# Three fills moved ahead in one scan stage, loads put behind a store, and the low part of the latent stages' weights made by a negated copy and an accumulating DMA

## The chip, the cores and the metric

The kernel runs on one core of a Trainium2 chip. Its metric is the device time of one execution in microseconds; the text gives the median of several executions. The engines are TensorE (PE, with its weight loads as PEld), VectorE (DVE), ScalarE (ACT), GpSimd (POOL) and SyncE (SP). SP and POOL issue the DMA transfers that matter here.

## The reference, cut to what matters

Two layers work on 512 latent tokens of 1024 channels, with 256 context tokens in front. The even layer has an RWKV-7 scan in both directions and a gated short convolution side by side:

```python
rc, kc, vc, zac, bc, cc, xc, zbc = jnp.split(hc @ w_in, EVEN_SPLITS, axis=-1)
yac, S_f, S_b = rwkv_seq(rwkv_prep(hc, ...), zero, zero, ...)      # the context: final states only
r, k, v, za, bg, cg, xb, zb = jnp.split(h @ w_in, EVEN_SPLITS, axis=-1)
ya, _, _ = rwkv_seq(rwkv_prep(h, r, k, v, ...), S_f, S_b, ...)     # the latent tokens
yb = bg * dwconv(cg * xb, sc_w, seg_len)
y = jnp.concatenate([ya * silu(za), yb * silu(zb)], axis=-1) @ w_out
```

Per token and head the scan does `S = S * w + (S @ -kk) (kk * a)^T + v k^T` and reads `S @ r`. The odd layer is a gated convolution of 31 taps with layer norm. Each layer is `x + gate * rms_norm(y)`, with shift, scale and gate from `silu(c) @ mod_w + mod_b`. Everything is fp32.

## The kernel before

*Exactness.* A product of fp32 matrices is made of three matmuls in a faster 32-bit format (`mm3`, every matmul of the trace is on line 57): each operand is split into a high part, a copy in that format, and a low part, the operand less the high part. For weights `hilo` does it: SP loads 128x512 fp32 (`wr...`, a half of a 1024x128 block of `w_in`), ACT copies it to `wh...` (line 129), DVE subtracts into `wl...` (line 130). `w_half` gives the buffers: two raw ones, three for each part. `load_w` loads both halves of a block, `proj` multiplies, 24 matmuls of 128x512 a block. The names end in the block and the half: `wlbg51` is the low part of half 1 of block `bg` 5.

*Stages.* The scan is done in chunks, as matmuls. Twelve stages follow a prologue: s=0 to 3 run the chain of the context's head groups (`chain_ctx`, four chunks), s=4 to 11 that of the eight latent groups (`chain_lat`, eight chunks). The chain is serial; after it in the text of a stage stands the work for coming stages, one letter each in `STAGE`: `O` the outputs of the next group (`po`), `S` its triangular solve (`solve`, in halvings on DVE with `Xl`, `Yl`, `xtmpl`), `M` the merge of the solved blocks on PE and DVE (`kdml`, `aml`, `Pml`, `uh`), `P` projections and the LoRA parts for the group after next (`prep_lat`), `L` the decays and keys (`light`, `ARl`, `BKl`, `kdl`), `H` its products within a chunk (`heavy`: `pal` masked by DVE into `E`, line 682, then `pbl` copied by ACT into `BKt`, line 695), `F` projections kept for later in DRAM (`fills`, through `psp`) and, from s=4, the group's end (`finish`: `Ol`, `osq`, `orq`, `ysp`), `C` one group of the short convolution (`conv_branch(s-3)`: blocks `cg`, `xb`, `bg` and the gate `zb`).

*Order.* A scheduler orders each engine's instructions by dependencies, by the order of the text, and by the text's anchors: `after(x)` and `issue_after(x)` let an instruction start in the order only behind `x`; `anchored` does so with a chunk of the chain. In `conv_branch` the weights' loads and their matmuls are anchored to chunks 0, 2, 7 and 6 of the chain. Each engine then runs its queue strictly in order. `rest` is the odd layer's (and the gate's) modulation, 17 steps laid between other work: of four matmuls each, on 128 rows of `mod_w` in four tiles of 512 columns; it loads the next group into the same tiles (`home`) from POOL. `between()` and `inner` are the places where a step may stand. `project` stores its result by POOL to `psp`.

*Names in the trace.* The trace leaves buffer numbers out, and one `pal` or `zoc` row of an engine's order stands for two of its records.

Of the kernel before, what the change touches and what calls it, by code (L numbers as in the profile page):

```python
# [15 lines left out]
P = 128  # L16
# [15 lines left out]
CONV_AFTER = (0, 2, 7, 6)  # L32
PA_ORDER = ((0, 1), (1, 0), (1, 1), (0, 0))
HEAVY = ("ANB", "ANBV")
STAGE = ("KLSMVHvF", "OPLSMHF", "OSPLMHFC")
FILL_R = (0, 0, 2, 3, 4, 4, 4, 4)
FILL_Z = (0, 1, 1, 1, 3, 3, 3, 3)
ZR = (slice(0, 64), slice(64, 128))
# [13 lines left out]
def kernel(ctx: ExitStack, tc: tile.TileContext, I: dict, out: bass.AP):  # L52
# [63 lines left out]
    w_in = I["ev_w_in"][0]  # L116
    wo = I["ev_w_out"][0]
    ORDER = list(range(8, 16)) + list(range(8))
    env = {"lo": V, "first": False}

    def bank(name, tag):
        return ps.tile([P, 512], F32, tag=tag, name=name, bufs=2 if tag in ("at", "zo") else 1)
# [255 lines left out]
    def lora(hp, w1, between):  # L378
        pwl, pal = (ps.tile([P, 512], F32, tag="zo", name=n, bufs=2) for n in ("pwl", "pal"))
        pwc = ps_at("pwc")  # L380
        for kt in range(KT):
            h1 = hp[kt][:, 1:771]
            dh = w("AR", f"dh{kt}")[:, 0:770]
            V.tensor_tensor(out=dh, in0=hp[kt][:, 0:770], in1=hp[kt][:, 2:772], op=ALU.add)
            for (zi, pl) in ((0, pwl), (1, pal)):
                xw = E1[:, (2 * kt + zi) % 4 * D : (2 * kt + zi) % 4 * D + 770]
                S.activation(xw, h1, AF.Copy, scale=owa[:, zi * 8 + kt : zi * 8 + kt + 1])
                V.scalar_tensor_tensor(out=xw, in0=dh, scalar=hwa[:, zi * 8 + kt : zi * 8 + kt + 1], in1=xw,
                                       op0=ALU.mult, op1=ALU.add)
                lhs = w1[zi][kt // 4][:, kt % 4].rearrange("p a b -> p (a b)")  # L390
                mm(pl, lhs, xw[:, 258:770], kt == 0, kt == KT - 1)
                mm(pwc[:, zi * CTX : (zi + 1) * CTX], lhs, xw[:, 0:CTX], kt == 0 and zi == 0, kt == KT - 1 and zi == 1)
            if kt % 2:
                between()
        lorl.extend([cvp.tile([P, SEQ], F32R, tag=f"{t}{z}", name=f"{t}{z}") for z in range(2)] for t in ("tanhl", "xal"))
        S.activation(lorc[0], pwc[:, 0:CTX], AF.Tanh)
        S.copy(lorc[1], pwc[:, CTX : 2 * CTX])
        for i, pl in enumerate((pwl, pal)):
            t, th = w("tmp", f"lor{i}"), w("tmp", f"lorh{i}", F32R)
            S.activation(t, pl, AF.Copy if i else AF.Tanh)  # L400
            S.copy(th, t)
            for z in range(2):
                rows, hr, lr = (slice(64 * x, 64 * x + 64) for x in (z, i, 1 - i))
                S.copy(lorl[i][z][hr], th[rows])
                V.tensor_tensor(out=lorl[i][z][lr], in0=t[rows], in1=th[rows], op=ALU.subtract)
# [4 lines left out]
    def w_half(src, name):  # L410
        raw = wp.tile([P, 512], F32, tag="wr", name="wr" + name, bufs=2)
        hi, lo = (wp.tile([P, 512], F32R, tag="w" + x, name=f"w{x}{name}", bufs=3) for x in "hl")
        with tc.high_priority() if env["first"] else nullcontext():
            return hilo(src, raw, hi, lo)

    def early_w(cb, raw):
        res = []
# [25 lines left out]
    def project(p, which, rc=None, between=None):  # L443
        nm = "rkv"[which] + str(p)
        wt = first_w.pop(nm) if nm in first_w else load_w(which * 8 + p, nm)
        if rc is not None:
            pc = (ps_at if nm in ("k0", "k1") else ps_mm)("pc" + nm)[:, :CTX]
            proj(wt, pc, (hch, hcl))
            shifted(pc, rc, p, which)
            if between:  # L450
                between()
        pl = ps_mm("pl" + nm)
        proj(wt, pl, hlat)
        flip["at"] ^= 1
        tag = ("cg", "yb")[flip["at"]]
        rl = cvp.tile([P, SEQ], F32, tag=tag, name="l" + nm)
        shifted(pl, rl, p, which)
        nc.gpsimd.dma_start(psp[p, which], rl)

    def state(lat, x):  # L460
        ps_ = [x] if lat else [2 * x, 2 * x + 1]
# [4 lines left out]
    def prep_ctx(b, between=None, st=None, kinds=(1, 2), inner=None, js=(0, 1)):  # L466
        st = st or state(False, b)
        for which in kinds:
            nm = "rkv"[which]
            if nm not in st:  # L470
                st[nm] = w("r_" if which == 1 and b % 2 else nm + "_", nm + st["nm"])
            for p, cs in [st["parts"][j] for j in js]:
                project(p, which, st[nm][:, cs], inner)
                if between:
                    between()
        return st
# [185 lines left out]
    def heavy(st, an=None):  # L662
# [5 lines left out]

        def pa():
            for gi, (z, g) in enumerate(PA_ORDER if lat else ((0, 0), (1, 0))):  # L670
                with anchored(an, ha[gi if lat else 2 * gi]):
                    AR, BK = st["AR"][z], st["BK"][z]
                    m, x = (4, P) if lat else (8, CH)
                    c0 = m * g
# [232 lines left out]

    def conv_branch(p, an=None):
        anchors = [None if an is None or x is None else an[x] for x in ((0, 2, 4, 6) if p == 7 else CONV_AFTER)]
        with after(anchors[0]):  # L910
            wt = load_w(40 + p, f"cg{p}")
            pcg = ps_mm(f"pcg{p}")
            proj(wt, pcg, hlat)
        cg = cvp.tile([P, SEQ], F32, tag="cg", name=f"cg{p}")
        S.copy(cg, pcg)
        with after(anchors[1]):
            wt = load_w(48 + p, f"xb{p}")
            pxb = ps_mm(f"pxb{p}")
            proj(wt, pxb, hlat)
        V.tensor_tensor(out=cx[:, :, 1:65], in0=ch3(pxb), in1=ch3(cg), op=ALU.mult)  # L920
        yb = cvp.tile([P, SEQ], F32, tag="yb", name=f"yb{p}")
        S.activation(ch3(yb), cx[:, :, 0:64], AF.Copy, scale=hc("sc_w", p))
        for j in (1, 2):
            V.scalar_tensor_tensor(out=ch3(yb), in0=cx[:, :, j : j + 64], scalar=hc("sc_w", 8 * j + p),
                                   in1=ch3(yb), op0=ALU.mult, op1=ALU.add)
        with after(anchors[2]):
            wt = load_w(32 + p, f"bg{p}")
            pbg = ps_mm(f"pbg{p}")
            proj(wt, pbg, hlat)
        V.tensor_tensor(out=yb, in0=pbg, in1=yb, op=ALU.mult)  # L930
        with after(anchors[3]):
            gz = gate(p, 56, "zb")
        V.tensor_tensor(out=yb, in0=yb, in1=gz, op=ALU.mult)
        nc.gpsimd.dma_start(ysp[8 + p], yb)
# [15 lines left out]
    def rest():  # L950
# [16 lines left out]
        for g in ((n + 1,) if n else (0, 1)):  # L967
            for q in ((0, 1, 2, 3), (3, 2, 1, 0))[g % 2] if g < 16 else ():
# [4 lines left out]
                    with tc.issue_after(env["last"].ins):  # L973
                        nc.sync.dma_start(home(g, q), src)
                else:
                    nc.gpsimd.dma_start(home(g, q), src)

    def rested(half_, acc):
        row = w("HP", f"mrow{half_}")
# [10 lines left out]
        if half_ == 0:  # L990
            V.memset(acc, 0.0)

    def fills(x):
        for p in range(8):
            if FILL_R[p] == x:
                project(p, 0)
            if FILL_Z[p] == x:
                gz = gate(p, 24, "za")
                nc.gpsimd.dma_start(psp[p, 3], gz)

    sts = [prep_ctx(0, rest)]
    whs, behind = first_w["spectra"]
    with tc.issue_after(behind):
        for ns, wh in whs:
# [19 lines left out]
    for s in range(12):  # L1024
# [7 lines left out]
        if s == 11:  # L1032
            finish(st)
            break
        env["first"] = s < 4
        for x in STAGE[(s >= 2) + (s >= 4)]:
            if x == "S":
                solve(sts[s + 1])
# [14 lines left out]
                light(sts[s + 2], st)  # L1053
            elif x == "H" and s < 10:
                heavy(sts[s + 2], st)
            elif x == "F":
                fills(s + 1)
                if s >= 4:
                    finish(st)
            elif x == "C":  # L1060
# [383 lines left out]
```

## Time and profile before

| | |
|---|---|
| median of 3 runs | 1385.95 us (1385.75, 1385.95, 1392.3) |
| the profiled execution | 1392.7 us, its span 1390.9 us |
| mean granted clock of PE | 0.992 of full speed |
| ACT busy, instructions | 745.3 us (54%), 1509 |
| POOL busy, instructions | 127.4 us (9%), 263 |
| DMA | 158.55 MB, mean 114 GB/s |
| stages in the span | s=2 350.6 to 411.7, s=3 to 482.4, s=4 to 540.4, s=5 to 601.3, s=6 to 659.3, s=7 to 717.7, s=8 to 775.4, s=9 to 833.5, s=10 to 878.4, s=11 to about 910 |

Busy times are those of one profiled execution; a row of waits tells the engine and line that waited, for which engine's tile, the time in all, how often, and the longest. A row of the timeline tells the start, the duration, the instruction, and in brackets the idle time before it and what ended it. A group's row tells its busy time, the mean of one in ns, then the idle time before and its releasers. The odd layer follows behind s=11.

### The profile page before, as it was taken

The numbers are of one execution on the slowest core, as the hardware profiler recorded it, in microseconds if no ns is written. First come the engines' busy times: TensorE is split into PE (matmuls) and PEld (weight loads), VectorE is DVE, ScalarE is ACT, GpSimd is POOL, SyncE is SP. The second block draws the span as 40 slices with busy tenths as digits, with TensorE's granted clock in tenths as the row PEclk, the third lists the DMA queues.
The fourth block names the chain that finished last, engine by engine and source line by source line (L and its number), as shares of the span: only waits on it lengthen the run. The fifth ranks groups of instructions, "written<-read, shape, count | busy, mean of one in ns | idle before, by whom it ended". The sixth has DMA issues, their size and how long they took to land.

```text
span 1390.9 us, 29758 instructions
## 1 busy us (share of the span) xinstructions
PE 1337.1 (96%) x11925; PEld 995.2 (72%) x11925; DVE 985.3 (71%) x2304; ACT 745.3 (54%) x1509; POOL 127.4 (9%) x263
## 2 busy tenths in 40 slices
PE   6989999999899999999999999999999999999998
PEld 2646777777677766676666676677777787788886
DVE  5846879868999599989999998557654653644323
ACT  6536366546756566665666755547742432554222
POOL 4123200001111010101101000010000000000000
PEclk9999999999999999999999999999999999999999
DMA  9855521222323312223222221578621322133232
GB/s 333 254 190 190 189 77 57 87 79 86 88 90 101 99 63 79 70 65 88 82 73 70 76 70 57 183 238 290 222 62 61 121 64 58 61 112 101 91 103 79
DMA packets 139756, 158.55 MB, mean 114 GB/s; under 512 B 15504, under 2 KB 104224, under 8 KB 139498
## 3 DMA queue, kind: packets, MB, share of 16 engines
q1 hardware_dynamic: 123152, 106.47, 24.7%
q0 software_dynamic: 15856, 49.12, 10.8%
q8 instruction: 94, 1.54, 0.5%
q10 hardware_dynamic: 608, 1.06, 0.2%
q14 instruction: 46, 0.37, 0.1%
HBM read 138.33 MB, written 18.28 MB: 113 GB/s over the span
## 4 chain that ended last, share of the span: by engine, by line
PE 66%; DVE 16%; ACT 6%; issue 6%; DMA 5%; SPq 0%; POOL 0%; DVEq 0%; ACTq 0%; POOLq 0%
PE pu L57 10%; PE pz L57 6%; PE f L57 6%; PE uh L57 4%; PE zol L57 4%; PE pcg L57 4%; PE o L57 4%; PE plk L57 3%; PE pxb L57 3%; PE plr L57 2%; PE plv L57 2%; PE pzb L57 2%; DVE E L682 2%; PE pck L57 1%; PE zoc L57 1%
## 5 line engine op out<-in xcount | busy, mean ns | idle before, releaser
L57 PE MATMUL o<-wh,y 128*128 128x512 f32 x248 | 79.7, 397 | 0.0
L739 DVE TENSOR_TENSOR xtmpl<-Xl,Yl 128x126 f32<-128x126 f32 (+22 forms) x248 | 61.9, 250 | 2.8
L741 DVE TENSOR_TENSOR Yl<-Yl,xtmpl 128x126 f32<-128x126 f32 (+22 forms) x248 | 61.9, 250 | 2.7
L1257 ACT CAST ah<-a 64x512 fp32r<-64x512 f32 x32 | 19.8, 618 | 72.6 <-DVE a L1252 72.2
L57 PE MATMUL zol<-UV,E 64*64 64x64 f32 (+1 forms) x1024 | 54.0, 221 | 0.0
L57 PEld LDWEIGHTS o<-wh,y 128*128 128x128 f32 x248 | 45.9, 188 | 9.5
L57 PE MATMUL o<-wl,y 128*128 128x512 f32 x124 | 49.6, 400 | 2.0 <-DVE wl L130 2.0
L57 PE MATMUL pal<-ARl,BKl 64*128 64x128 f32 x512 | 45.7, 298 | 5.8 <-DVE E L682 5.2
L57 PE MATMUL zol<-Hl,ARl 64*64 64x64 f32 x896 | 50.2, 230 | 0.7 <-DVE Hl L854 0.4
L847 ACT COPY UV<-uh 64x128 f32<-64x128 f32 x128 | 33.3, 260 | 32.5 <-PE uh L57 25.0
L57 PEld LDWEIGHTS zol<-Hl,ARl 64*64 64x64 f32 x896 | 34.9, 133 | 20.0 <-issue 15.1
L130 DVE TENSOR_TENSOR wl<-wr,wh 128x1024 fp32r<-128x1024 f32 x28 | 34.2, 1223 | 20.6 <-ACT wh L129 20.5
L57 PEld LDWEIGHTS pal<-ARl,BKl 64*128 64x128 f32 x512 | 36.1, 193 | 16.9 <-issue 10.2
L57 PEld LDWEIGHTS uh<-UV,BKt 128*64 128x64 f32 x704 | 26.3, 137 | 30.3 <-ACT UV L847 23.4
L1252 DVE TENSOR_TENSOR a<-pu,a 128x512 f32<-128x512 f32 x16 | 11.0, 690 | 47.7 <-PE pu L57 45.4
L57 PEld LDWEIGHTS zol<-UV,E 64*64 64x64 f32 (+1 forms) x1024 | 42.2, 136 | 2.8 <-ACT UV L847 2.1
L682 DVE TENSOR_TENSOR E<-pal,maskE 128x512 f32<-128x512 f32 x64 | 43.0, 682 | 0.5 <-PE pal L57 0.3
L1209 DVE SCALAR_TENSOR_TENSOR pr<-px,dbe,What 119x512 f32<-119x512 f32 x32 | 22.6, 747 | 26.6 <-PE px L57 26.6
L129 ACT CAST wh<-wr 128x1024 fp32r<-128x1024 f32 x28 | 29.6, 1057 | 21.3 <-PE o L57 10.7
L854 DVE SCALAR_TENSOR_TENSOR Hl<-uh,PCl,HPl 128x64 f32<-128x64 f32 x112 | 26.4, 277 | 19.4 <-PE uh L57 9.2
L57 PE MATMUL uh<-UV,BKt 128*64 128x64 f32 x704 | 36.3, 232 | 3.3 <-ACT UV L847 2.0
L57 PEld LDWEIGHTS uh<-Ol,E 64*64 64x64 f32 x512 | 19.9, 133 | 24.5 <-ACT Ol L841 17.3
(996 smaller groups left out, 4206.1 us busy)
## 6 DMA issues: line engine op xcount, KB each, us to landing
wr<-in_ev_w_out_dram SPq DMA_DIRECT2D x28, 512.0 KB, 5.2
mwr<-in_mod_w_dram POOLq DMA_DIRECT2D x28, 256.0 KB, 4.3
wrv<-in_ev_w_in_dram SPq DMA_DIRECT2D x16, 256.0 KB, 3.1
ectx<-in_mod_w_dram POOLq DMA_DIRECT2D x16, 256.0 KB, 4.2
wrr<-in_ev_w_in_dram SPq DMA_DIRECT2D x16, 256.0 KB, 2.9
wrza<-in_ev_w_in_dram SPq DMA_DIRECT2D x16, 256.0 KB, 2.8
wrcg<-in_ev_w_in_dram SPq DMA_DIRECT2D x16, 256.0 KB, 2.8
wrxb<-in_ev_w_in_dram SPq DMA_DIRECT2D x16, 256.0 KB, 3.0
```

The costliest lines, as they stand in the source:

```text
L57: env["pe"] = T.matmul(o, lhsT, rhs, start=start, stop=stop)
L129: S.copy(hi, raw)
L130: env["lo"].tensor_tensor(out=lo, in0=raw, in1=hi, op=ALU.subtract)
L682: st["ev"].append(V.tensor_tensor(out=E[:, h, z * NLAT + c0 : z * NLAT + c0 + m, :], in0=pas[h], in1=maskE[:, z * (1 + h) : z * (1 + h) + ...
L739: V.tensor_tensor(out=tv, in0=X[:, :i, i : i + 1].to_broadcast([P, i, m]), in1=Y[:, i : i + 1, c0:].to_broadcast([P, i, m]), op=ALU.mult)
L741: V.tensor_tensor(out=Y[:, :i, c0:], in0=Y[:, :i, c0:], in1=tv, op=ALU.add)
L847: u_ = S.copy(UV[ZR[1 - h], i : 2 * nch - i : 2 * nch - 1 - 2 * i, ZR[h]], uh[ZR[1 - h], 0:2, :])
L854: h_ = V.scalar_tensor_tensor(out=Hn[:, z, :], in0=uh[:, 2 + z, :], scalar=PC[z][:, i : i + 1], in1=HP[:, z, :], op0=ALU.mult, op1=ALU.add)
L1209: V.scalar_tensor_tensor(out=pr[s][:NPROD], in0=px[s][:NPROD], scalar=dbe[:, 0:1], in1=What[:, n * 512 : n * 512 + 512], op0=ALU.add, op1= ...
L1252: V.tensor_tensor(out=a, in0=pp[1], in1=a, op=ALU.mult)
L1257: S.copy(ahl[s][hr], a[hr])
```

## The change

Five edits. (1) In s=2 (the letter `f`) the first three of the five fills, the projection R3 and the gates Z4 and Z5, are written ahead of `heavy`, and every `pal` group of that `heavy` but the first is put behind the last matmul of these fills. (2) In `lora` the place for a modulation step behind the second of eight slices is dropped, and one opens inside the second value projection of the context's first block. (3) `rest`'s loads by POOL stand behind the last store of `project`. (4) In `conv_branch` the loads of `cg`, `xb` and `bg` stand outside the anchors, which hold the matmuls alone. (5) From s=4 on, in `w_half`, the low part is made without DVE: ACT copies the high part, ACT writes its negative into the low part's buffer, and a DMA issued by POOL adds the same weights from DRAM into that buffer.

```diff
-STAGE = ("KLSMVHvF", "OPLSMHF", "OSPLMHFC")
+STAGE = ("KLSMVHvF", "OPLSMfHF", "OSPLMHFC")
...
-            if kt % 2:
+            if kt % 2 and kt > 1:
                 between()
...
         with tc.high_priority() if env["first"] else nullcontext():
-            return hilo(src, raw, hi, lo)
+            if not env["added"]:
+                return hilo(src, raw, hi, lo)
+            nc.sync.dma_start(raw.rearrange("p (k c) -> p k c", c=P), src)
+            S.copy(hi, raw)
+            S.activation(lo, hi, AF.Copy, scale=-1.0)
+            nc.gpsimd.dma_start(lo.rearrange("p (k c) -> p k c", c=P), src.bitcast(F32R), accum_op=ALU.add)
+            return hi, lo
...
-        nc.gpsimd.dma_start(psp[p, which], rl)
+        env["store"] = nc.gpsimd.dma_start(psp[p, which], rl)
...
-                project(p, which, st[nm][:, cs], inner)
+                project(p, which, st[nm][:, cs], inner if b or (p, which) == (1, 2) else None)
...
-                with anchored(an, ha[gi if lat else 2 * gi]):
+                with anchored(an, ha[gi if lat else 2 * gi]), after(st.get("hold") if gi else None):
...
+        wt = load_w(40 + p, f"cg{p}")
         with after(anchors[0]):
-            wt = load_w(40 + p, f"cg{p}")
             pcg = ps_mm(f"pcg{p}")
...
-                    nc.gpsimd.dma_start(home(g, q), src)
+                    with tc.issue_after(env["store"].ins):
+                        nc.gpsimd.dma_start(home(g, q), src)
...
-    def fills(x):
+    def fills(x, first=0, last=None):
...
-    sts = [prep_ctx(0, rest)]
+    sts = [prep_ctx(0, rest, inner=rest)]
...
+        env["added"] = s >= 4
...
+            elif x == "f" and s == 2:
+                fills(s + 1, 0, 3)
+                sts[s + 2]["hold"] = env["pe"].ins
             elif x == "F":
-                fills(s + 1)
+                fills(s + 1, 3 if s == 2 else 0)
```

`xb` and `bg` move out of their anchors as `cg` does. `env["added"]` starts as False. In `fills` the pairs of kind and group are listed in the old order and cut to `[first:last]`.

PE in s=2, behind the chain's last output of the context (`zoc3_0`). `pal01..` are the products of `heavy` for the first latent group, `pza5` the gate Z5. Before:

```order
L57 MATMUL zoc3_0_4480<-UV010_1746,ectx_123 64x64 x8
L57 MATMUL pal0101_4173<-ARl01_4005,BKl01_4006 128x128
L57 MATMUL pal0100_4172<-ARl01_4005,BKl01_4006 128x128
...
L57 MATMUL pza5_4368<-hlh0_117,whza50_4357 128x512
L57 MATMUL pza5_4368<-hll0_118,whza50_4357 128x512
L57 MATMUL pza5_4368<-hlh0_117,wlza50_4358 128x512
...
L57 MATMUL pal0111_4185<-ARl01_4005,BKl01_4006 128x128
L57 MATMUL pal0110_4184<-ARl01_4005,BKl01_4006 128x128
```

The same place after:

```order
L57 MATMUL zoc3_0_4480<-UV010_1746,ectx_123 64x64 x8
L57 MATMUL pza5_4251<-hlh0_117,whza50_4240 128x512
...
L57 MATMUL pza5_4251<-hll1_448,whza51_4246 128x512
L57 MATMUL pza5_4251<-hlh1_447,wlza51_4247 128x512
L57 MATMUL pal0101_4297<-ARl01_4005,BKl01_4006 128x128
L57 MATMUL pal0100_4296<-ARl01_4005,BKl01_4006 128x128
...
L57 MATMUL pza6_4409<-hlh0_117,whza60_4398 128x512
```

Before, eight rows of `pal` stand right behind the output and seven `pza5` matmuls between two `pal` groups; after, all 24 `pza5` matmuls stand ahead of the eight, and Z6 begins behind them.

DVE in a latent stage (s=8, the chain of latent group 4), from the chain's step `Hl4_6` on. `Yl5`, `xtmpl5` are the solve of the next group, `kdml5` and `aml5` the start of its merge, `E100` the masks of the group after next. Before:

```order
L854 SCALAR_TENSOR_TENSOR Hl4_6_8907<-uh0_125,PCl41_7436,HPl4_6_8875 128x64
L867 TENSOR_TENSOR Ol4_8672<-zol4_6_8883,Ol4_8672 128x2x64
L741 TENSOR_TENSOR Yl5_8944<-Yl5_8944,xtmpl5_8945 128x6x13
...
L130 TENSOR_TENSOR wlbg51_9426<-wrbg51_9424,whbg51_9425 128x512
L867 TENSOR_TENSOR Ol4_8672<-zol4_7_8915,Ol4_8672 128x2x64
L739 TENSOR_TENSOR xtmpl5_8945<-Xl5_8943,Yl5_8944 128x56
L682 TENSOR_TENSOR E100_4157<-pal6010_9186,maskE_107 128x512
L741 TENSOR_TENSOR Yl5_8944<-Yl5_8944,xtmpl5_8945 128x4x14
L682 TENSOR_TENSOR E100_4157<-pal6011_9187,maskE_107 128x512
```

After:

```order
L860 SCALAR_TENSOR_TENSOR Hl4_6_8939<-uh0_125,PCl41_7452,HPl4_6_8907 128x64
L873 TENSOR_TENSOR Ol4_8704<-zol4_6_8915,Ol4_8704 128x2x64
L637 SCALAR_TENSOR_TENSOR BKl61_9135<-al61_9119,iPl61_9123 128x8x64
...
L753 STREAM_TRANSPOSE kdml5_9141<-Yl5_8976 128x32x16
L754 STREAM_TRANSPOSE aml5_9142<-kdml5_9141 128x512
L758 COPY E110_4899<-kdml5_9141 32x16x32
L873 TENSOR_TENSOR Ol4_8704<-zol4_7_8947,Ol4_8704 128x2x64
L758 COPY E110_4899<-kdml5_9141 32x16x32
L688 TENSOR_TENSOR E100_4281<-pal6010_9218,maskE_107 128x512
```

The subtraction is gone, the solve's last steps stand ahead of `Hl4_6`, and the merge's transposes, which stood behind the masks, now stand ahead of the first one.

POOL in a latent stage (before s=7, after s=8, which look alike but for the change); the `wl` rows are the accumulating transfers, `ysp` and `psp` are in DRAM. Before:

```order
L483 DMA kl6_9011<-psp_79 128x512
L483 DMA rl6_9015<-psp_79 128x512
L894 DMA gz3_8503<-psp_79 128x512
L520 DMA lwrl6_9018<-in_ev_w2_dram 64x2x128
L520 DMA lwrl6_9018<-in_ev_a2_dram 64x2x128
...
L732 DMA Yl5_8944<-in_unit_dram 128x512
```

After:

```order
L419 DMA wlbg50_9456<-in_ev_w_in_dram 128x4x128
L489 DMA kl7_9880<-psp_79 128x512
L489 DMA rl7_9884<-psp_79 128x512
L419 DMA wlbg51_9463<-in_ev_w_in_dram 128x4x128
L738 DMA Yl6_9813<-in_unit_dram 128x512
L900 DMA gz4_9364<-psp_79 128x512
L526 DMA lwrl7_9887<-in_ev_w2_dram 64x2x128
L526 DMA lwrl7_9887<-in_ev_a2_dram 64x2x128
...
L419 DMA wlzb50_9496<-in_ev_w_in_dram 128x4x128
L526 DMA lwrl7_9887<-in_ev_a2_dram 64x2x128
L419 DMA wlzb51_9503<-in_ev_w_in_dram 128x4x128
```

Eight `wl` rows a stage have come into the queue, the second `bg` half behind `rl`, the `zb` halves behind `Yl` and `gz`; `Yl` has moved ahead of `gz` and `lwrl`.

More of the change, by code (lines that the diff above doesn't have):

```diff
@@ L118 @@
     ORDER = list(range(8, 16)) + list(range(8))
-    env = {"lo": V, "first": False}
+    env = {"lo": V, "first": False, "added": False}
     def bank(name, tag):
@@ L915, in conv_branch @@
         S.copy(cg, pcg)
+        wt = load_w(48 + p, f"xb{p}")
         with after(anchors[1]):
-            wt = load_w(48 + p, f"xb{p}")
             pxb = ps_mm(f"pxb{p}")
@@ L925, in conv_branch @@
                                    in1=ch3(yb), op0=ALU.mult, op1=ALU.add)
+        wt = load_w(32 + p, f"bg{p}")
         with after(anchors[2]):
-            wt = load_w(32 + p, f"bg{p}")
             pbg = ps_mm(f"pbg{p}")
@@ L991, in rested @@
             V.memset(acc, 0.0)
-    def fills(x):
-        for p in range(8):
-            if FILL_R[p] == x:
+    def fills(x, first=0, last=None):
+        for kind, p in [(kind, p) for p in range(8) for kind in "RZ" if (FILL_R, FILL_Z)[kind == "Z"][p] == x][first:last]:
+            if kind == "R":
                 project(p, 0)
-            if FILL_Z[p] == x:
+            else:
                 gz = gate(p, 24, "za")
                 nc.gpsimd.dma_start(psp[p, 3], gz)
-    sts = [prep_ctx(0, rest)]
+    sts = [prep_ctx(0, rest, inner=rest)]
     whs, behind = first_w["spectra"]
```

## The prediction

> **What bounds the kernel now.** I read the page's busy shares and slices first, then each stage's stretch, then what TensorE (PE) waits for inside the stages, then the chain of waits in one stage.
>
> ```profile
> PE 1337.1 (96%) x11925; PEld 995.2 (72%) x11925; DVE 985.3 (71%) x2304; ACT 745.3 (54%) x1509; POOL 127.4 (9%) x263
> DVE  5846879868999599989999998557654653644323
> ```
>
> The page says PE, at 96% of the span. But DVE stands at nine tenths in slices 11 to 28 of 40, where the scan's stages lie, so there two engines are near full at once and the short waits of PE are what can be won. Next the stretches, one per stage (stage s=2, then latent stages s=4 to s=10; columns: stretch, PE, PEld, DVE, ACT, POOL busy, PE's granted clock, DMA share, GB/s), then s=6 cut into the part with the serial chain and the dense part behind it.
>
> ```profile
> 350.60:411.70 61.10, 55.34 (x627) 41.95 (x626) 57.16 (x157) 37.38 (x77) 6.75 (x12) 0.94 0.28 85
> 482.40:540.40 58.00, 55.69 (x774) 39.25 (x773) 53.58 (x161) 37.51 (x90) 6.72 (x12) 1.00 0.24 74
> 540.40:601.30 60.90, 58.19 (x773) 42.06 (x772) 55.80 (x167) 37.79 (x91) 6.73 (x12) 0.94 0.25 72
> 601.30:659.30 58.00, 55.46 (x773) 39.22 (x772) 53.22 (x155) 37.68 (x90) 6.21 (x12) 1.00 0.27 76
> 659.30:717.70 58.40, 55.80 (x775) 39.17 (x774) 53.95 (x157) 37.70 (x90) 6.81 (x13) 1.00 0.26 75
> 717.70:775.40 57.70, 55.97 (x774) 39.21 (x773) 53.06 (x153) 37.21 (x89) 7.15 (x13) 1.00 0.27 79
> 775.40:833.50 58.10, 55.89 (x775) 39.66 (x774) 54.28 (x158) 37.95 (x91) 3.24 (x6) 1.00 0.22 66
> 833.50:878.40 44.90, 44.73 (x637) 31.28 (x636) 34.17 (x105) 19.67 (x56) 2.15 (x4) 1.00 0.19 59
> 601.30:633.50 32.20, 31.79 (x440) 20.84 (x439) 28.66 (x92) 22.49 (x64) 2.67 (x5) 1.00 0.21 62
> 633.50:659.30 25.80, 23.67 (x335) 18.38 (x334) 24.56 (x63) 15.19 (x27) 3.53 (x7) 1.00 0.33 93
> ```
>
> PE idles 2.31, 2.71, 2.54, 2.60, 1.73 and 2.21 us in s=4 to s=9, together 14.1, and 0.17 in s=10. In s=6 nearly all of it, 2.13, lies in the dense part, where DVE is busy 24.56 of 25.80 us (95%) and ACT only 59%; in the chain's part PE is idle for 0.41. So in the dense part DVE sets the pace. What PE waits for in s=4 to s=9 (us, times, longest), and pieces of the chain of waits in the dense part of s=6 (start, us, what):
>
> ```profile
> PE pbl L657 <- ACT BKt L695: 2.8, 5, 1.0
> PE uh L57 <- DVE aml L748: 2.7, 4, 1.0
> PE po L57 <- DVE Ol L887: 2.4, 3, 1.1
> ...
> 638.27 0.59 DVE wlbg L130
> ...
> 651.08 0.60 DVE wlcg L130
> ```
>
> The waits are short and of several kinds, most on DVE. These two are the first and last of four subtractions on s=6's chain that the change takes off DVE, 2.4 us together.
>
> **The change part by part.** *The weights' low parts (conv branches 1 to 7).* Removed: 56 DVE subtractions, one per half of a 256 KB weight block, eight a stage. Added: 56 negated copies on ACT and 56 accumulating transfers issued by POOL.
>
> ```profile
> L130 DVE TENSOR_TENSOR wlbg<-wrbg,whbg 128x512 fp32r<-128x512 f32 x14 | 9.6, 684 | 0.3 <-PE pxb L57 0.3
> L129 ACT CAST whxb<-wrxb 128x512 fp32r<-128x512 f32 x14 | 8.6, 614 | 6.0 <-PE pzb L57 2.1 <-issue 1.8 <-ACT UV L712 1.4
> L883 ACT ACTIVATE osq<-Ol 128x512 f32<-128x512 f32 x7 | 4.4, 633 | 3.8 <-DVE Ol L867 3.8
> ```
>
> DVE loses 56 x 0.684 = 38 us, 5.5 a full stage. What of this reaches the end is bounded from above in two ways: by the pieces on the chain (2.4 in s=6), and by the idle time of PE in the dense part (2.13). The removal cannot pay in the chain's part, where PE has nothing to give. I take 1.9 a stage, nine tenths of the smaller bound because other DVE work of the same part moves up into the places: the transposes that `uh` waits for and the finish's `Ol`, both in the list of waits above, stand earlier in the new order. Six stages give −11.4; s=10 gives −0.5 at most from its own 0.17 and the first weights of the stage, and I take −0.5: together −12. Below, the bound is 0 (PE's idle time turns into other waits), above it −14.
>
> The negated copy is the size of `osq`, 128x512 with a scale on ACT: 56 x 0.63 = 35 us more of ACT, 5.1 a stage. ACT goes from 37.5 of 58 us to 42.6, 73%; in the dense part from 15.2 to about 18.4 with five of the eight copies. Behind each copy on ACT's queue stand the copies that `pbl` waits for, 2.8 us already, and the copies of `UV`. I take +2, a delay of half a copy in each of the seven stages, with 0 and +5 as ends (one full delay of 0.63 in each of the seven stages would be 4.4).
>
> POOL's issue is seen under a DVE as busy as it gets (s=7), and two of its transfers and two of SP's have times from issue to landing:
>
> ```profile
> 684.80 0.54 POOL L483 DMA_DIRECT2D kl<-psp  x1 [20.92 <-DVE Yl L741]
> 699.83 0.56 POOL L732 DMA_DIRECT2D Yl<-in_unit_dram  x1 [5.59 <-DVE orq L496]
> wrcg<-in_ev_w_in_dram SPq DMA_DIRECT2D x16, 256.0 KB, 2.8
> kl<-psp POOLq DMA_DIRECT2D x8, 256.0 KB, 3.2
> wr<-in_ev_w_out_dram SPq DMA_DIRECT2D x28, 512.0 KB, 5.2
> x<-in_x_dram POOLq DMA_DIRECT2D x4, 512.0 KB, 8.9
> ```
>
> 56 issues at 0.56 are 31 us more of POOL, 4.5 a stage on 6.7 of 58: nothing, since POOL is 80% idle. No row of the trace shows a transfer that adds into its destination. It carries the 256 KB and must also fetch what lies there; the bounds are 2.8 (a plain load of as many bytes) and 8.9 (POOL's slowest row of 512 KB). I take 5.2, the 512 KB row at the DMA share of the stages, because twice the bytes is the nearest likeness. Is that early enough? The halves have three buffers each. The casts of the dense part show the pace at which halves are used:
>
> ```profile
> 635.55 0.62 ACT L129 CAST whzb<-wrzb 128x512 fp32r<-128x512 f32 x1 [0.33 <-PE pxb L57]
> ...
> 649.09 2.51 ACT L701 COPY Nt<-E 32x512 f32<-32x512 f32 x4 [0.27 <-DVE E L682]
> ...
> 659.27 0.62 ACT L129 CAST whxb<-wrxb 128x512 fp32r<-128x512 f32 x1 [0.69 <-ACT UV L712]
> ```
>
> From the first to the fifth cast is 23.7 us, 5.9 a half. A half may be cast when the one three before it is used up, and is needed when the two between are used up too: 2 x 5.9 = 11.8 us later. Of those go at worst 2.5 (the `Nt` copies ahead on ACT), 0.62 + 0.63 for the two copies and 0.56 for the issue, so the transfer may take 7.5 us. At 5.2 it is hidden, with 2.3 to spare; above 7.5 a half takes (F + 4.3)/2 us, F being the transfer. That spare time also covers POOL's order: the second `bg` half stands behind `rl`, the `zb` halves behind `Yl`, `gz` and `lwr`. Every transfer there has a wait, so a late one stalls the weights; I price this under the rivals. SP's loads stay as many, and the raw buffer comes free one ACT copy later instead of one DVE subtraction: nothing, as the buffers' loads land in 2.8 of 5.9 us. DMA's share rises by 56 x 256 KB twice over, small on 0.25.
>
> [...]
>
> *The early fills at s=2.* R3, Z4 and Z5 move ahead of heavy's later `pal` groups. PE's timeline there:
>
> ```profile
> 381.45 2.08 PE L57 MATMUL pal<-ARl,BKl 64*128 64x128 f32 x16 [3.90 <-DVE E L682]
> ...
> 384.05 0.63 PE L57 MATMUL pza<-hll,whza 128*128 128x512 f32 x1
> 384.48 0.63 PE L57 MATMUL pza<-hlh,wlza 128*128 128x512 f32 x1
> ...
> 386.74 1.63 PE L57 MATMUL pal<-ARl,BKl 64*128 64x128 f32 x16
> ...
> 388.65 0.40 PE L57 MATMUL pza<-hlh,wlza 128*128 128x512 f32 x1
> 388.88 0.40 PE L57 MATMUL pza<-hlh,whza 128*128 128x512 f32 x1
> ...
> 390.13 1.16 PE L57 MATMUL pal<-ARl,BKl 64*128 64x128 f32 x16
> ```
>
> PE waits 3.90 us for the mask step that frees a bank of `pal`, with ready `pza` matmuls queued behind, and then runs slow to about 388: the next `pza` follows after 0.43 instead of 0.23 (7 of them stand there, 1.4 us lost), and two `pal` groups take 2.08 and 1.63 instead of 1.16 (1.4 lost), 2.8 together. In the new order 24 `pza` matmuls (24 x 0.23 = 5.5 us) stand there first and cover the wait. Upper bound: 3.9 + 2.8 = 6.7. DVE has only 3.9 us idle in the stage of 61.1, and the moved groups make `E` of the first latent group later, which the solve in s=3 then wants; so at worst all comes back, 0. I take −4.5: the wait less 1.3 that is paid later on DVE, plus two thirds of the slow steps (1.9). [...]
>
> *Modulation in the middle of the second block's value projections, and the step dropped from lora.* The count of steps stays. Four of its matmuls come to stand in this gap:
>
> ```profile
> 80.94 0.76 PE L57 MATMUL plv<-hlh,whv 128*128 128x512 f32 x1 [3.56 <-DVE lv L440]
> ...
> 88.00 0.60 PE L57 MATMUL uh<-mwbtanhl,s 128*2 128x512 f32 x2
> ...
> 88.86 1.04 PE L57 MATMUL uh<-mwr,s 128*2 128x512 f32 x8
> ...
> PE uh L57 <- DMA mwbxal<-in_mod_w_dram: 0.2, 1, 0.2
> ```
>
> The moved step runs from 88.00 to 88.86, where the next one starts: 0.9 us, laid into 3.56 us of idle. What is left of the gap may be short enough to spare some of the slow steps behind it, 1.4 us if they are as many as at s=2. I take −1; ends 0 and −2.3.
>
> *Loads behind the store.* A group of four loads moves past one store on POOL at 0.55 each; PE waited 0.2 us for such a load in all. Nothing. *The conv loads without their anchors.* They only let SP, and ACT's casts, run earlier; the free buffer holds them. Nothing beyond the term on ACT.
>
> Sum: −12 + 2 − 4.5 − 1 = −15.5. The profiled execution took 1392.7 (span 1390.9 and 1.8 around it); the sum makes it 1377.2. It lay 6.75 above the median of the runs, 1385.95; taken off, 1370.5, forecast as 1370.
>
> **The rivals.** *All of DVE's relief pays.* If the idle of the dense part was only the visible share (a matmul is drawn with 0.40 where the next follows after 0.23, so each break in PE's row hides 0.17; I estimate six such a stage), six stages could give 14.1 + 6, with s=5's slow clock (0.94 in its row, 60.9 us against 58) gone: 2.9 more. With s=2 at its −6.7 and the early gap at −2.3: −32, 1354. For it: DVE at 95% in the dense part. Against: the DVE work that remains there, 21 of 24 us, is on the same chain.
>
> *PE is the bound and nothing of DVE's relief shows.* Matmul work is the same and PE is 96% busy; freed DVE time goes idle, ACT's 35 us cost the 2, and changes between kinds of matmul on PE grow a little. Left are s=2 and the early gap: −5.5 + 2 = −3.5, about 1382; no change.
>
> *The accumulated low part is late (slower).* If a transfer takes three passes of `kl`'s 3.2, 9.6 us, a half of the dense part takes (9.6 + 4.3)/2 = 6.95 instead of 5.9: 1.05 x 5 halves x 7 stages = +37, on −15.5: +21, 1407. It eats the gain above F = 8.4 us, and makes the kernel slower by over 0.5% from 8.8. POOL's order does the same: an issue that waits some 3 us behind `Yl` adds as much to F. For it: the 8.9 us row, and the waits on POOL of 5.59 and more. Against: the 2.3 us to spare, and that the loads on POOL at the stages' DMA share take 3.2.
>
> **How the numbers follow.** About 0.5% (6.9 us) can be told from no change, so faster is below 1379 and slower above 1393. Forecast: 0.50. All of the relief: 0.17. PE the bound: 0.20. Late accumulation: 0.13. The forecast reaches over 1379 at its ends of s=2 and ACT, so 0.05 of its half goes to the same and nearly all else of it is faster: faster 0.45 + 0.17 + 0.07 (the part of the third that goes below 1379) = 0.69; the late case splits 0.03 same and 0.10 slower; same 0.05 + 0.13 + 0.03 = 0.21; slower 0.10. The range: from 1353, just under the first rival, to 1392, which holds the third and what the late case leaves below break-even; outside are the 0.10 of slower and some 0.08 below. The forecast's own range is 1362 to 1380.
>
> **What would show it.** Right: at s=2 no wait of 3 us or more before `pal` and no slow `pza`; stages s=4 to s=9 of about 56 us with DVE near 85% and ACT near 73%; no PE wait on a transfer into `wl`. The sum fails if PE or `zb`'s matmuls wait for `wlzb` or `wlbg` (transfers over 7.5 us, or POOL issues standing behind `Yl`), if PE's waits on `BKt` and `UV` grow past 5 us (the ACT term), or if s=3 grows by what s=2 loses.

## The result: slower by 0.63%, and where the time went

The changed kernel takes 1396.34 us (median of 11 runs), the kernel before 1386.55 (11 runs beside them): ratio 1.0063, 95% interval 1.0043 to 1.0084. The forecast was 1370, its range 1353 to 1392.

The first part of the page after (busy time and share of each engine, instructions):

```profile
PE 1346.5 (96%) x11925; PEld 999.6 (71%) x11925; DVE 969.9 (69%) x2248; ACT 776.7 (55%) x1565; POOL 202.1 (14%) x319
```

DVE has 56 instructions less and ACT and POOL 56 more, as the change says. ACT rose by 31 us (35 forecast), POOL by 75 (31 forecast), and DVE fell by 15 (38 forecast). The stages of the changed kernel (s=2 to s=10; columns as in the prediction), and s=3 of before, which was not shown:

```profile
347.30:410.30 63.00, 57.18 (x629) 42.90 (x628) 52.89 (x140) 36.95 (x77) 6.75 (x12) 0.92 0.29 86
410.30:485.50 75.20, 69.74 (x702) 53.50 (x701) 58.76 (x142) 44.61 (x90) 9.89 (x16) 1.00 0.34 95
485.50:550.40 64.90, 61.69 (x759) 44.15 (x758) 53.88 (x171) 42.34 (x98) 17.71 (x21) 0.87 0.51 104
550.40:608.20 57.80, 55.70 (x773) 39.33 (x772) 51.15 (x146) 42.18 (x98) 16.23 (x19) 1.00 0.55 107
608.20:666.70 58.50, 56.33 (x775) 39.37 (x774) 52.76 (x151) 42.45 (x98) 17.64 (x21) 1.00 0.56 111
666.70:725.80 59.10, 56.26 (x773) 39.48 (x772) 52.34 (x148) 42.09 (x98) 17.38 (x21) 1.00 0.56 109
725.80:784.70 58.90, 56.37 (x773) 39.53 (x772) 52.39 (x149) 42.14 (x98) 17.45 (x21) 1.00 0.55 110
...
843.30:888.90 45.60, 44.41 (x637) 32.01 (x636) 28.74 (x92) 23.43 (x64) 11.38 (x11) 1.00 0.50 93
...
411.70:482.40 70.70, 69.01 (x686) 52.80 (x685) 55.33 (x126) 42.97 (x86) 7.42 (x14) 1.00 0.33 101
```

Against the stages of before: s=2 is 63.0 long (61.1), s=3 75.2 (70.7), s=4 64.9 (58.0, now at a granted clock of 0.87), s=5 57.8 (60.9, whose slow clock is gone), and the later ones are 0.5 to 1.2 longer each. DVE is busy for 89 to 90% of s=6 to s=8 (92% before) and ACT for about 72%, and the stages are no shorter for it. The DMA share went from 0.25 to 0.55. The profiled execution of the changed kernel took 1401.95, 5.6 over its median, so its stages are to be read for the kind of loss; its size stands in the experiments.

Two losses show in these stages. What PE waits for in s=2, then in s=4 (us, times, longest):

```profile
PE pza L57 <- DVE lr L446: 3.8, 1, 3.8
...
PE pbl L663 <- DVE E L688: 2.4, 1, 2.4
```

At s=2 the long wait has stayed and only changed its name: the gate's matmuls, which were to cover it, wait themselves, for DVE's shift of R3 (`lr`). At s=4 a new wait has come. Its history is in the timelines of POOL, ACT, DVE and PE there:

```profile
520.36 1.37 POOL L419 DMA_DIRECT2D wlzb<-in_ev_w_in_dram  x1
521.15 1.20 POOL L526 DMA_DIRECT2D lwrl<-in_ev_a_dram  x1
...
527.41 0.62 ACT L529 CAST lwhl<-lwrl 128x512 fp32r<-128x512 f32 x1 [4.06 <-DMA lwrl<-in_ev_a_dram]
527.94 0.63 ACT L418 ACTIVATE wlzb<-whzb 128x512 fp32r<-128x512 f32 x1
...
528.07 0.69 DVE L530 TENSOR_TENSOR lwll<-lwrl,lwhl 128x512 fp32r<-128x512 f32 x1 [2.02 <-ACT lwhl L529]
...
529.88 0.68 DVE L688 TENSOR_TENSOR E<-pal,maskE 128x512 f32<-128x512 f32 x1
...
531.32 1.12 PE L663 MATMUL pbl<-ident,BKl 64*128 64x64 f32 x16 [2.45 <-DVE E L688]
...
532.00:536.00 4.00, 4.00 (x50) 3.03 (x46) 4.00 (x8) 3.90 (x7) 0.57 (x1) 0.50 0.47 66
544.00:548.00 4.00, 4.00 (x70) 3.45 (x65) 1.53 (x5) 1.68 (x3) 0.00 (x0) 0.50 0.55 115
```

The last of the four LoRA weight loads (`lwrl`) stands behind an accumulating transfer on POOL and lands late. ACT's copy of it waits 4.06 us with the next negated copy queued behind; DVE's low part of it waits for ACT with the masks queued behind; PE waits 2.45 us for a mask, and then runs at half clock, as the last two rows (stretches of 4 us, the clock third from the end) show for the first and the fourth of four stretches in a row: 16 us of it. Two things make the load late: it is issued 1.8 us behind the third load (at 519.32), where 0.6 is the distance of the others, and ACT gets it 6.3 us after its issue. In s=5 to s=8 the order weighs more: the transfer ahead itself waits 1.7 to 2.2 us for ACT's negated copy, with the load behind it (below, s=5). All over s=4 to s=9 ACT now waits 17.3 us for this load and waited 4.6 before; it lands in 4.2 us after issue, before in 3.0:

```profile
587.56 1.33 POOL L419 DMA_DIRECT2D wlzb<-in_ev_w_in_dram  x1 [1.68 <-ACT wlzb L418]
588.37 1.15 POOL L526 DMA_DIRECT2D lwrl<-in_ev_a_dram  x1
...
ACT lwhl L529 <- DMA lwrl<-in_ev_a_dram: 17.3, 5, 4.1
...
ACT lwhl L523 <- DMA lwrl<-in_ev_a_dram: 4.6, 3, 1.9
...
wlzb<-in_ev_w_in_dram POOLq DMA_DIRECT2D x14, 256.0 KB, 4.7
lwrl<-in_ev_a_dram POOLq DMA_DIRECT2D x16, 64.0 KB, 4.2
...
lwrl<-in_ev_a_dram POOLq DMA_DIRECT2D x16, 64.0 KB, 3.0
```

### The profile page after: what moved, and what is told of

It reads as the page before. It is cut to its first block, busy times and chain, and to the rows that moved or that the text cites. A ratio compares the mean times of both kernels' runs of the same rounds, so it can differ in the third digit from the quotient of the medians.

```text
span 1400.2 us, 29856 instructions
## 1 busy us (share of the span) xinstructions
PE 1346.5 (96%) x11925; PEld 999.6 (71%) x11925; DVE 969.9 (69%) x2248; ACT 776.7 (55%) x1565; POOL 202.1 (14%) x319
## 4 chain that ended last, share of the span: by engine, by line
PE 69%; DVE 12%; ACT 7%; issue 6%; DMA 5%; POOL 1%; SPq 0%; DVEq 0%; ACTq 0%; POOLq 0%
PE pu L57 11%; PE pz L57 6%; PE f L57 6%; PE uh L57 5%; PE o L57 4%; PE zol L57 3%; PE plk L57 3%; PE pcg L57 3%; PE pxb L57 3%; PE plv L57 2%; PE plr L57 2%; PE pck L57 2%; DVE xtmpl L745 1%; PE pzb L57 1%; DVE Yl L747 1%
## 5 line engine op out<-in xcount | busy, mean ns | idle before, releaser
L57 PEld LDWEIGHTS zol<-Hl,ARl 64*64 64x64 f32 x896 | 34.9, 133 | 21.2 <-issue 12.5
L853 ACT COPY UV<-uh 64x128 f32<-64x128 f32 x128 | 33.3, 260 | 23.9 <-PE uh L57 19.4
```

The lines of the kernel that those rows point to most:

```text
L57: env["pe"] = T.matmul(o, lhsT, rhs, start=start, stop=stop)
L853: u_ = S.copy(UV[ZR[1 - h], i : 2 * nch - i : 2 * nch - 1 - 2 * i, ZR[h]], uh[ZR[1 - h], 0:2, :])
```

## The experiments

All were timed in five rounds beside the kernel before; ratios are against it, with 95% intervals. Theory A: the accumulation costs, through POOL's order. Theory B: the early fills cost. Theory C: chance in the clock.

### The change without the accumulation, and the accumulation alone

```diff
-        env["added"] = s >= 4
+        env["added"] = False
```

> The change without the accumulation: DVE subtracts in every stage, the other four edits stay. Theory A (the accumulation costs: its place in POOL's queue makes the LoRA weights late, and a stall of 2.45 us in s=4 leads to a slow clock): 10 to 15 us faster than the changed kernel, 1380 to 1386 us. Theory B (the early fills cost: they only move the wait of s=2 and make s=3 longer): like the changed kernel, 1392 to 1397. Theory C (slow clock at random): no difference beyond the spread.

Measured 1400.93, ratio 1.0088 (1.0065 to 1.0110), above the ranges of both theories. Theory A alone falls: without the accumulation the change is no faster. The other way round, only edit 5 on the kernel before:

> The kernel before with the accumulation alone. Theory A: slower than before, 1392 to 1398 us, with ACT's lwhl copies waiting some 18 us in all for the lwrl transfers. Theory B: as before or some us faster, 1380 to 1387.

1393.02, 1.0039 (1.0025 to 1.0054). A has its share too, about 5.4 us; ACT waits 14.6 us for `lwrl` in s=4 to s=9, some less than expected. The two parts do not simply add up: 1.0079 (the fills, below) and 1.0039 would give 1.0118, above the interval of the whole.

### The early fills, with three, two and four

Only edit 1 on the kernel before:

> The kernel before with the early fills alone. Theory A: within 3 us of before, 1383 to 1389. Theory B: slower by 5 or more, 1391 to 1396, s=2 and s=3 together some 6 us longer. As I forecast this part: 1382.

1398.91, 1.0079 (1.0064 to 1.0095): 11 us, theory B and above its range, and by the medians more than the whole change costs (the two intervals overlap). Both intervals, of the fills and of the accumulation, are clear of 1, so chance (theory C) does not explain them. Its stages s=2 to s=4, and behind them those of the kernel with the modulation edits alone (below), whose clock is at 0.97 or above in all stages:

```profile
345.06:408.95 63.89, 57.98 (x627) 43.60 (x627) 52.97 (x140) 36.86 (x77) 6.74 (x12) 0.89 0.28 84
408.95:485.00 76.05, 69.77 (x704) 53.57 (x704) 60.08 (x144) 43.39 (x88) 7.38 (x14) 1.00 0.31 92
485.00:546.92 61.92, 56.74 (x757) 40.58 (x756) 56.32 (x170) 36.92 (x90) 6.73 (x12) 0.94 0.23 70
...
348.28:408.99 60.71, 54.04 (x627) 41.00 (x626) 57.04 (x158) 37.46 (x78) 6.74 (x12) 0.97 0.28 86
408.99:479.65 70.66, 68.93 (x686) 52.79 (x685) 55.31 (x126) 42.87 (x86) 7.40 (x14) 1.00 0.34 101
479.65:537.63 57.98, 55.71 (x774) 39.23 (x773) 53.59 (x161) 37.47 (x90) 6.71 (x12) 1.00 0.25 74
```

The three stages are 201.9 long against 189.4. DVE idles 10.9 us in s=2 (63.89 less 52.97) instead of 3.7, and its work comes later: 60.1 us busy in s=3 for 55.3, 56.3 in s=4 for 53.6. PE's long wait in s=2, then DVE's first late masks and the solve behind them, of the three fills; then the last mask and the solve of the kernel without them:

```profile
375.62 0.80 PE L57 MATMUL pza<-hlh,whza 128*128 128x512 f32 x1 [3.85 <-DVE lr L440]
...
393.65 0.69 DVE L766 COPY ectx<-uh 32x512 f32<-32x512 f32 x1 [2.12 <-ACT ectx L766]
394.36 1.29 DVE L682 TENSOR_TENSOR E<-pal,maskE 128x512 f32<-128x512 f32 x2
399.08 1.29 DVE L682 TENSOR_TENSOR E<-pal,maskE 128x512 f32<-128x512 f32 x2 [3.44 <-PE pal L57]
402.85 2.05 DVE L733 STREAM_TRANSPOSE Xl<-Nt 128x1024 f32<-128x1024 f32 x1 [1.71 <-ACT Nt L701]
...
389.78 0.69 DVE L682 TENSOR_TENSOR E<-pal,maskE 128x512 f32<-128x512 f32 x1
393.60 2.12 DVE L733 STREAM_TRANSPOSE Xl<-Nt 128x1024 f32<-128x1024 f32 x1 [0.47 <-ACT Nt L701]
```

Counted from the start of s=2 the solve of the first latent group starts at 402.85 − 345.06 = 57.8 us instead of 393.60 − 348.28 = 45.3. DVE, which in the kernel before fed on the early `pal` groups, has to wait for PE and for the context's merge instead, and the solve comes 12.5 us late. I read the loss as this: the solve misses the free places of DVE in s=2, and its work meets the work of s=3 and s=4.

A slow clock is part of this loss, at least in these two executions. PE is busy 5.8 us longer in the three stages (184.5 us for 178.7) with as many matmuls (2088 and 2087), at granted clocks of 0.89 and 0.94 in s=2 and s=4 against 0.97 and 1.00; the other 6.7 us are PE idle. The runs do not separate the slow stretches from the waits that they follow.

With R3 and Z4 alone ahead (`fills(s + 1, 0, 2)`), 5 matmuls of Z5 stand ahead of the second `pal` group instead of 24; with four (`0, 4`), 48.

> The early fills alone, but only R3 and Z4 (Z5 stays behind): 5 matmuls of Z5 stand ahead of the second pal group instead of 24. If the 24 starve DVE, which then idles some 7 us in s=2 and is late with the solve: 1385 to 1390, s=2 to s=4 together within 2 us of before. If another part of the edit costs: 1395 to 1399 as with three fills.

1390.17, 1.0020 (0.9999 to 1.0040), s=2 to s=4 190.5 long: within 1.2 of the kernel without early fills. The median lies 0.2 above its range and far below the other one, so it is Z5 ahead of the `pal` groups that costs; R3, Z4 and the hold on the masks' groups behind them cost 2.8 us by the ratio, and may cost nothing.

> Four early fills instead of three, alone: 48 matmuls of gates (Z5, Z6) stand ahead of the second pal group, where three fills put 24 and two put 5. If they keep DVE waiting for the masks' inputs, 24 more at 0.23 are 5.5 us: 1401 to 1407, masks ending some 5 us later than with three. If three fills only hit an unlucky order: 1390 to 1399.

1400.16, 1.0090 (1.0067 to 1.0113): between the two ranges, hardly more than with three. The cost does not grow with the count. The last mask starts 54.9 us after the start of s=2, with three fills 54.6, without the edit 41.5. Without it the masks are done before the context's merge begins (`kdmc`, at 42.1); with three and with four fills DVE's step `ectx` of that merge, behind a wait of 2.12 and of 2.19 us, stands ahead of the last four and the last six masks. So the loss looks like one of falling behind the merge, for which 24 matmuls are enough; that place was not tried by itself.

### The modulation edits alone

Edits 2 and 3 on the kernel before:

> The kernel before with the modulation edits alone (a step inside the value projection, none behind the second slice of lora, POOL's loads behind the store). All theories: 1 to 4 us faster than before, 1382 to 1385, since the changed kernel is 3.8 us ahead when s=0 begins.

1387.03, 0.9994 (0.9983 to 1.0005): missed. No change can be told. In its trace PE waits nowhere 0.3 us or more between 60 and 120 us, so the gap of 3.56 us is closed as the edit meant; but the same gap was 1.84, 2.32 and 2.57 us in three kernels that do not have the edit (three fills alone, no low part, LoRA loads moved). The profiled execution of before had an unusually long one.

### What DVE's relief is worth: no low part, and the negated copy without the transfer

Both leave out part of the computation, as their expectations say. The first is the accumulation alone less its last two steps:

```diff
             S.copy(hi, raw)
-            S.activation(lo, hi, AF.Copy, scale=-1.0)
-            nc.gpsimd.dma_start(lo.rearrange("p (k c) -> p k c", c=P), src.bitcast(F32R), accum_op=ALU.add)
-            return hi, lo
+            return hi, hi
```

> The kernel before with DVE's subtraction left out in the latent stages and nothing put in its place: the high part stands for the low part in the product (its output is not the reference's; the matmuls are as many). It bounds what DVE's relief can give. If DVE sets the pace of the dense parts, as I forecast: 10 to 14 us faster than before, 1373 to 1377. If PE is the bound there: 0 to 4 us, 1383 to 1387.

1382.81, 0.9973 (0.9958 to 0.9988): 3.7 us (1.7 to 5.8), at the fast end of what was expected if PE is the bound, and far from 1373 to 1377. The second drops the transfer only:

> The accumulation alone, less its transfers: ACT still writes the negated copy, POOL adds nothing, so the low part stays the negated high part. If the transfers cost (POOL's order, late lwrl): as fast as the kernel without low parts, up to 3 us above it. If ACT's copies in the chain cost: like the accumulation alone, 1391 to 1394.

1383.30, 0.9964 (0.9945 to 0.9983), 5.0 us (2.4 to 7.6). ACT's 35 us cost nothing that can be told. Stages s=4 to s=9 in one stretch, without edit (the modulation edits alone) and without the low part:

```profile
479.70:828.10 348.40, 334.36 (x4633) 235.95 (x4632) 323.64 (x947) 225.60 (x536) 36.80 (x66) 1.00 0.25 74
476.80:823.60 346.80, 334.77 (x4633) 235.51 (x4632) 312.92 (x906) 225.71 (x535) 37.09 (x66) 1.00 0.25 75
```

The first stretch holds 49 subtractions of line 130, the second 2. 47 fewer at 0.684 are 32 us (six other steps came into the stretch, so DVE's count fell by 41), but DVE's busy time fell by 10.7 and PE's idle time from 14.0 to 12.0. The stretch itself is only 1.6 us shorter, so in these two executions not even the 3.7 us are seen in it. The gap between 32 and 10.7 has a cause that rows of DVE show, of before (a subtraction among others) and of the changed kernel (the same kind of small steps in a row):

```profile
638.10 0.17 DVE L885 TENSOR_SCALAR orq<-orq 128x8 f32<-128x8 f32 x1
638.17 0.69 DVE L130 TENSOR_TENSOR wlbg<-wrbg,whbg 128x512 fp32r<-128x512 f32 x1
638.77 0.17 DVE L741 TENSOR_TENSOR Yl<-Yl,xtmpl 128x16 f32<-128x16 f32 x1
...
705.42 0.17 DVE L502 TENSOR_SCALAR orq<-orq 128x8 int32<-128x8 int32 x1
705.63 0.17 DVE L504 TENSOR_TENSOR orq<-orq 128x8 f32<-128x8 f32 x1
705.83 0.17 DVE L505 TENSOR_TENSOR orq<-orq 128x8 f32<-128x8 f32 x1
```

In these rows an independent subtraction begins 0.07 after the start of a step of 0.17; a step that needs the one before begins after 0.20. The subtractions stood between dependent steps and hid part of their latency: taken away, they free less than their own 0.60. The sizes bear this out. In the two stretches the subtractions had 29 us of DVE's busy time, and other steps took about 19 of it back. More than half of that is the solve: each of its small steps (`xtmpl`, `Yl`, some 385) filled 0.19 us up to the next start on DVE with the subtractions there and 0.22 without, about 11 us together (over s=4 to s=9 of before and of the changed kernel 0.20 and 0.23).

Between DVE's 10.7 us and PE's 2.0 lies a second gap: a stage's dense part became shorter, its chain part longer. In s=6 they are 24.4 and 33.3 us without the low part, 25.4 and 32.6 with it. PE's waits for `Hl` in the chain went from 0.5 to 3.3 us in six stages (with the low part, then without):

```profile
PE zol L57 <- DVE Hl L854: 0.5, 2, 0.2
...
PE zol L57 <- DVE Hl L858: 3.3, 6, 0.7
```

Part of what DVE's relief frees goes into waits on single results.

### The LoRA weights on SP

```diff
-                    nc.gpsimd.dma_start(raw[64 * b : 64 * b + 64, i], ...)
+                    nc.sync.dma_start(raw[64 * b : 64 * b + 64, i], ...)
```

First with the accumulation alone, then with nothing else as the control:

> The accumulation alone, with the lwrl loads issued by SP instead of POOL, so that none stands behind an accumulating transfer. If the late lwrl is what the accumulation costs: 1380 to 1387, no wait of ACT's lwhl over 2.5 us. If DMA traffic or ACT's copies cost: 1390 to 1394 as with POOL's loads.

1386.57, 0.9991 (0.9974 to 1.0009): the accumulation's 5.4 us are gone, though its transfers (4.7 to 5.1 us) and the DMA share (0.56) are as with POOL's loads. ACT's waits for these loads in s=4 to s=9 fell from 14.6 to 4.3 us, the longest 2.8.

> The kernel before with nothing but the lwrl loads moved to SP (the control for the accumulation with these loads on SP). ACT's lwhl waits 5.3 us for them in all before, so: within 2 us of before, 1385 to 1389. If the move pays by itself, as much as 6 us, then it was not the accumulating transfers ahead of these loads that cost.

1388.54, 1.0003 (0.9982 to 1.0024). The move pays only where accumulating transfers stand ahead. Whether what counted was the earlier issue or the faster landing, the move does not tell. Then the changed kernel without its fills, the same with the loads on SP, and the whole changed kernel with them on SP:

> The changed kernel with the fills and the masks' hold put back as before; modulation, conv loads and accumulation stay. If the parts add up (accumulation alone 5.4 us slower, modulation 0.8 faster): 1391 to 1394, some 3 to 5 us faster than the changed kernel. If the fills and the accumulation overlap in what they cost: as slow as the changed kernel, 1396.

1389.36, 1.0010 (0.9987 to 1.0034): faster than either range. Why it is not as slow as the accumulation alone stays open: ACT waits 13.9 us for `lwrl` here and 14.6 there, and the two intervals overlap.

> The same with the lwrl loads on SP: what is left of the change when both costs are taken out. If late LoRA weights are what the accumulation costs: 1382 to 1387, at or a little under before. If the conv loads without anchors cost: 1388 to 1392.

1384.98, 0.9985 (0.9962 to 1.0009), within its range. The loads without anchors (edit 4) were not tried alone; this kernel holds them, the modulation edits and the accumulation with the loads on SP, and is not told apart from the accumulation with these loads on SP alone (1386.57).

> The whole changed kernel with only the lwrl loads moved to SP. If the 2.45 us stall of s=4 and the slow clock behind it come from the late lwrl: no such stall, s=4 under 62 us, 1388 to 1393. If they come from the fills alone: unchanged, 1394 to 1398.

1390.76, 1.0024 (1.0000 to 1.0047), as expected. Its ACT waits for `lwrl` and its stages s=3 and s=4:

```profile
ACT lwhl L529 <- DMA lwrl<-in_ev_a_dram: 4.4, 4, 3.1
...
408.19:485.26 77.07, 71.35 (x704) 54.55 (x704) 58.80 (x142) 44.65 (x90) 7.67 (x12) 0.98 0.32 94
485.26:542.38 57.12, 54.87 (x758) 38.58 (x757) 52.21 (x166) 42.20 (x98) 14.80 (x16) 1.00 0.58 115
```

s=4 is 57.1 instead of 64.9, with the full clock and without the wait of 2.45; s=3 keeps what the fills cost. It is also shorter than s=4 with the fills alone (61.9): there, where the fills have put work on DVE, the accumulation's relief pays. That fits the two parts not adding up, but rests on single profiles. The ratios say the same: the fills cost 0.79% on the kernel before, but 0.53% on the changed kernel without them (1.0063 against 1.0010) and 0.39% where the loads are on SP (1.0024 against 0.9985).

In three pairs the move of the loads to SP took off 0.48% (accumulation alone), 0.25% (changed kernel without the fills) and 0.39% (whole changed kernel), and nothing in the control. Only in the first are the two intervals apart; the other two point the same way.

### What is left: the other loads, and the adding itself

```diff
-            nc.gpsimd.dma_start(t, psp[p, which])
+            nc.sync.dma_start(t, psp[p, which])        # and h0d, psp[p, 3], unit likewise
```

> The change without the early fills and with every load of the latent stages (lwrl, kl, rl, vl, h, gz, Yl) on SP: POOL keeps the stores and the accumulating transfers. If POOL's order is what the accumulation still costs: 1380 to 1383, some 3 us faster than with lwrl alone on SP. If the traffic costs, or SP's own order takes POOL's place: 1384 to 1390.

1386.43, 0.9992 (0.9975 to 1.0010): no gain over 1384.98.

The other leaves the adding out, as its expectation says:

```diff
-            nc.gpsimd.dma_start(lo..., src.bitcast(F32R), accum_op=ALU.add)
+            nc.gpsimd.dma_start(lo..., src.bitcast(F32R))
```

> The accumulation alone with lwrl on SP, where the transfer into the low part writes without adding (the low part becomes the raw weight). If the adding itself costs (a longer transfer, a longer issue): 1382 to 1384, issues of 0.55 us and transfers near 3.2 us. If any transfer of 256 KB from POOL costs as much: 1386 as with adding.

1385.48, 0.9983 (0.9964 to 1.0002), between the two expectations. One issue of it against 1.37 in the changed kernel, and its transfer against 4.7:

```profile
518.50 0.77 POOL L419 DMA_DIRECT2D wlzb<-in_ev_w_in_dram  x1 [3.67 <-ACT wlzb L418]
...
wlzb<-in_ev_w_in_dram POOLq DMA_DIRECT2D x14, 256.0 KB, 3.4
```

The adding makes the row of an issue 0.6 us and a transfer 1.3 us longer. The row overlaps the next one, though: the issue behind an adding one starts 0.79 us after it (520.36 to 521.15 in the changed kernel), and the whole row without adding is 0.77, so in these rows it holds POOL's queue hardly longer than that. The time does not tell the adding: the intervals of this, of the adding (0.9974 to 1.0009) and of no transfer at all (0.9945 to 0.9983) overlap. What the accumulation still costs with the loads on SP stays open, between 0 and some 4 us. No version is told apart from the kernel before on the fast side, except those that leave the low part out.

## Why the prediction was wrong

- **The low parts (−12).** The step that failed is "in the dense part DVE sets the pace", from DVE's 95% there. The term was mis-sized: leaving the subtractions out altogether is worth 3.7 us, 5.0 with ACT's copies in their place, 7.6 at the end of that interval. DVE's busy share counted latencies as well as work (32 us of subtractions taken out took 10.7 off it), and PE's idle time could not be had by one engine's relief (14.0 to 12.0 us). The rival that says PE is the bound named this, with 0.20.
- **The end of DVE's nine tenths.** The prediction put it at slice 28; the row quoted there has it at 24, with slices 14 and 18 below.
- **ACT (+2).** Nothing that can be told; its end of 0 was right.
- **The transfer.** 4.7 us against 5.2 taken, and hidden by the three buffers as worked out: no wait of PE on a transfer into `wl` shows in the changed kernel. The row of POOL's issue took 1.31 (median of `wlbg`) and not 0.56, though the next issue started 0.79 behind its start (520.36 to 521.15). DMA's share, "small on 0.25", rose to 0.55; no run shows that this cost time. Without adding, the row of an issue took 0.77 and the landing 3.4.
- **POOL's order.** The prediction counted as "nothing, since POOL is 80% idle" what stands behind an issue, and priced only a late `wl`. What was late is what the accumulating transfers were put in front of, the fourth `lwrl` load; its wait went over ACT's queue to DVE's, to PE's. The slower rival had the queue but the wrong load, and forecast 21 us where the accumulation alone cost 5.4. So the 0.10 given to "slower" stood for something that did not happen.
- **The early fills (−4.5).** The step that failed is that the 24 `pza` matmuls "cover the wait": they wait for the same DVE (`lr`, 3.85). The bound "at worst all comes back, 0" failed too: DVE idles 7.2 us more, the solve starts 12.5 late, and three stages lose 12.5 in the profiled executions, part of it to a slow clock: +11 by the medians. No rival had a loss here, though the prediction named "if s=3 grows by what s=2 loses" as a sign; it grew by 5.4, beside 3.2 more in s=2.
- **Modulation (−1).** −0.8, interval from −2.4 to +0.7: the gap closes as forecast, with `plv` matmuls 0.23 apart behind it (78.67 to 79.37) where before has them 0.43 apart (81.51 to 83.64), and the gain cannot be told from nothing. Its end of −2.3 rested on a gap that other executions show shorter.
- **The sum against one execution.** The profile of before was 6.75 over the median, with a slow clock in s=5 and a long gap at 81 us. The rival of a large gain counted the former as a gain of the change.

## What to carry to other kernels

Before an instruction is put in front of a wait to cover it, read what that instruction waits for itself: if it is the same late engine, the wait only changes its name, and what stood there before and fed that engine comes later. A queue that is 80% idle still has an order; list for every issue put into it what then stands behind, who waits for that on which in-order engine, and what is queued there. And a busy share near 95% is not yet a bound: leave the work out altogether in one run, and see what it is worth.

## What the runs showed of the hardware

- In the changed kernel a wait of 2.45 us was followed by 16 us of half clock with PE busy throughout (4.00 of 4.00 in the stretches quoted). Longer waits were followed by less: one of 3.56 us (before, to 80.94) by 2.7 us of matmuls 0.43 apart instead of 0.23, one of 3.85 us (three fills alone, to 375.62) by 4.4 us of them. In these three the length of the wait does not tell how long the slow steps last.
- A transfer of 256 KB that adds into its destination shows a row of 1.31 us for POOL's issue, with the next issue 0.79 us after its start in the rows shown, and takes 4.7 us to land; the same one without adding shows a row of 0.77 and takes 3.4. With eight adding ones a stage the DMA share over s=4 to s=9 is 0.56, with none 0.25. With the LoRA loads on SP the queue that holds them (q0) moved 61.70 MB with adding and without; its packets took 19.1% of the 16 engines' span with adding, 15.9% without.
- On DVE a step of 0.17 us was followed by an independent subtraction 0.07 us after its start, by a step that needs its result after 0.20, in the rows shown. So taking 47 subtractions of 0.684 us out of a row of dependent steps took 10.7 us off DVE's busy time, not 32.
